# A four-layer decoder trunk: the convolution's diagonal taps issued in halves around the next projection, summed in accumulator banks, and the output weights split after the first statistics

## The chip, the cores and the metric

One core of one Trainium2 chip runs the whole program. The time is the device time of one execution in microseconds (us), as the median of several executions. TensorE is called PE, VectorE DVE, ScalarE ACT, GpSimd POOL and the engine that issues the transfers SP, as in the profile. Each engine takes its own instructions in the order in which they were compiled; between engines there are only semaphores.

## The reference

Four layers, each a token mixer and a feed-forward block, in float32, for 256 positions and 1024 channels. The mixer of layers 0 and 3 is the causal convolution, the only code that the change touches:

```python
def conformer_conv(x, w_in, b_in, w_dw, b_dw, ln_g, ln_b, w_out, b_out):
    h = x @ w_in + b_in
    a, g = jnp.split(h, 2, axis=-1)
    h = a * jax.nn.sigmoid(g)
    h = causal_dwconv(h, w_dw, b_dw)          # 31 taps for each channel
    h = jax.nn.silu(layer_norm(h, ln_g, ln_b))
    return h @ w_out + b_out
```

## The kernel before

Weights come from memory as `raw` tiles of 1 MB (pool of 4) and are split into a high half `whi` (ACT, L87) and a low half `wlo` (DVE, L88), so that PE can make a float32 product out of three faster ones (L105 to L107). PE's order is the order of the source. DVE's, ACT's and SP's is made by a scheduler when the program is built; `tc.issue_after` tells it only that an instruction has to stand behind another.

In `conv` (layer 0 with `j` = 0, layer 3 with `j` = 1) the channels are in four pairs of 128-channel blocks, numbered `pr` = 0 to 3; `n` = 0, 1 is the block inside a pair. For a pair:

- `project(pr)`: 96 products into two PSUM banks, for n = 0 first (gate, then value), then n = 1.
- `glu(pr)`: for each n a sigmoid on ACT (`sg`, L429) and a product on DVE (`chp`, L430), then 16 shifted copies into the tile `h4` (shown as `h`), some on ACT (L422) and some on DVE (L424). `h4` and the diagonal weights `dg` (`diagonals`, DVE, L404) have two buffers each: those of pair 2 are those of pair 0, and those of pair 3 those of pair 1. POOL clears the left border of each `h4` (L413).
- `rest(pr)`: the last 3 to 7 of the 31 taps by plain multiply-add, the first of them on ACT (L446), the others on DVE (L448), into `cv`.
- `taps(pr)`: the other taps as products with diagonal matrices on PE (L461), 24 or 28 for each n (two records each in the trace), and one addition on DVE that puts their sum onto `cv` (L464).
- `to_tokens(pr, t)`: transposes of `cv` on PE (L469) into the accumulator banks `tm`, for token tiles t = 0, 1.

After all four pairs DVE takes the layer norm's statistics (`stats`, L475), and `normalise` (L478), `turn_z` (PE, L483), `activate` and the output product follow for token tile 0 and then 1. Pairs 2 and 3 go through `taps` by token tile. The matrix of the output product is four units `ws`; the first two are loaded and split just before `glu(3)`, the last two after the second statistics. The dictionary `order` holds the last copies of `glu(3)`, behind which later splits stand.

PSUM has eight banks here: four in the rotating pool `mm` (`bank()`), four named accumulators (`acc_bank(t, h)`).

Of the kernel before, what the change touches and what calls it, by code (L numbers as in the profile page):

```python
# [12 lines left out]
AF = mybir.ActivationFunctionType  # L13
# [14 lines left out]
ALPHA = (2 * DEPTH) ** 0.25  # L28
EPS = 1e-5


GROUPS = ((6, 6, 7, 7), (6, 6, 6, 7))
ACT_COPIES = ((11, 16, 12, 9), (7, 15, 13, 8))
GMIN, GMAX = min(map(min, GROUPS)), max(map(max, GROUPS))


@with_exitstack
def trunk(ctx: ExitStack, tc: tile.TileContext, ins, out):
# [18 lines left out]
    def bank():  # L57
        return mmp.tile([P, 512], F32, name="mm", tag="mm")
# [4 lines left out]
    def accs():  # L63
        return [[acc_bank(t, h) for h in range(2)] for t in range(2)]
# [32 lines left out]
    def unit_rows(w, k0, parts=1):  # L97
        return halves(load(w[k0 * P:(k0 + 2) * P, :].rearrange("(k p) n -> p k n", p=P), 2, D), 2, D, parts)
# [264 lines left out]
    def conv(j, prm, lv, turn, nxt, w_first):  # L363


        with tc.tile_pool(name=f"conv{j}", bufs=2) as p:
# [4 lines left out]
            def project(pr, ws=None):  # L371

                parts = 4 if pr == 1 and j == 0 else 1
                ws = ws or conv_weights(j, pr, parts)
                bks = [bank() for n in range(2)]
                if pr:
                    ws = [halves(w, KT, 256, parts) for w in ws]
                    for n in range(2):
                        for s in range(2):
                            proj_cols(bks[n][:, s * T:(s + 1) * T], ws[s], n)  # L380
                    return bks
                for t in range(2):
                    for n, s in ((0, 0), (1, 0), (0, 1)) if t == 0 else ((0, 0), (0, 1), (1, 0)):
                        if (t, n, s) == (1, 1, 0) and j == 0:
                            first["prm"] = prm(acc_bank(1, 1))
                        proj_cols_f32(bks[n][:, s * T:(s + 1) * T], ws[s], n, t, turn if (t, n, s) == (0, 0, 1) else None)
                    if j == 0:
                        proj_cols_f32(bks[1][:, T:], ws[1], 1, t)
                if j:
                    proj_cols(bks[1][:, T:], halves(ws[1][:, :, P:], KT, P), 0)  # L390
                return bks
# [16 lines left out]
            def glu(pr, bks):  # L408

                hp = p.tile([P, 2, PAD + T], F32, name="chp", tag="chp", bufs=3)  # L410
                pool.memset(hp[:, :, 0:PAD], 0.0)
                h4 = p.tile([P, 2, 4, PAD + T], F32, name="h4", tag="h4")
                pool.memset(h4[:, :, :, 0:PAD], 0.0)  # L413
                last = {}

                def copies(a, b):
                    for r in range(4):
                        for s in range(4):
                            src, dst = hp[32 * r:32 * r + 32, a:b, PAD:], h4[32 * s:32 * s + 32, a:b, r, PAD - s:PAD - s + T]
                            i = 4 * r + s  # L420
                            if i * ACT_COPIES[j][pr] // 16 != (i + 1) * ACT_COPIES[j][pr] // 16:
                                last["act"] = act.activation(out=dst, in_=src, func=AF.Identity).ins  # L422
                            else:
                                last["dve"] = dve.tensor_copy(dst, src).ins  # L424

                for n in range(2):
                    c = 2 * pr + n
                    sg = p.tile([P, T], F32, name="sg", tag="sg")
                    act.activation(out=sg, in_=bks[n][:, :T], func=AF.Sigmoid, bias=b_in[:, 8 + c:9 + c])  # L429
                    dve.scalar_tensor_tensor(out=hp[:, n, PAD:], in0=bks[n][:, T:], scalar=b_in[:, c:c + 1], in1=sg, op0=ALU.add, op1=ALU.mult)  # L430
                    if pr == 3:
                        copies(n, n + 1)
                if pr < 3:
                    copies(0, 2)
                return hp, h4, last

            def rest(pr, hp):

                cv = p.tile([P, 2, T], F32, name="cv", tag="cv", bufs=3)
                k0 = 4 * GROUPS[j][pr]  # L440
                for k in range(k0, KW):
                    for n in range(2):
                        c = 2 * pr + n
                        x, w, y = hp[:, n, k:k + T], w_rest[:, (k - 4 * GMIN) * 8 + c:(k - 4 * GMIN) * 8 + c + 1], cv[:, n, :]
                        if k == k0:
                            act.activation(out=y, in_=x, func=AF.Identity, scale=w, bias=b_dw[:, c:c + 1])  # L446
                        else:
                            dve.scalar_tensor_tensor(out=y, in0=x, scalar=w, in1=y, op0=ALU.mult, op1=ALU.add)  # L448
                return cv

            def taps(pr, t0=0, t1=T, ns=(0, 1)):
                if (pr, t0) not in sums:
                    sums[pr, t0] = bank().rearrange("p (n t) -> p n t", n=2)
                ps = sums[pr, t0][:, :, 0:t1 - t0]
                for n in ns:
                    for g in reversed(range(GROUPS[j][pr])):

                        first_g = g == GROUPS[j][pr] - 1
                        a = t0 if first_g else max(t0, PAD - 4 * g - 3)
                        for r in range(4):  # L460
                            pe.matmul(out=ps[32 * r:32 * r + 32, n, a - t0:], lhsT=dg[pr][:, 4 * n + r, g, :], rhs=h4[pr][:, n, r, 4 * g + a:4 * g + t1],  # L461
                                      start=first_g, stop=g == 0)
                y = cv[pr][:, ns[0]:ns[-1] + 1, t0:t1]
                dve.tensor_tensor(out=y, in0=ps[:, ns[0]:ns[-1] + 1, :], in1=y, op=ALU.add)  # L464
# [7 lines left out]

            def stats(t, h):
                with tc.issue_after(order["dve"]):
                    dve.bn_stats(out=st[t][:, h, :], in_=tm[t][h])  # L475

            def normalise(t, h, mv, rs):
                dve.tensor_scalar(out=z[t][:, h * 512:(h + 1) * 512], in0=tm[t][h], scalar1=mv[:, 0:1], scalar2=rs, op0=ALU.subtract, op1=ALU.mult)  # L478
# [19 lines left out]
            hp[0], h4[0], _ = glu(0, b0)  # L498
            cv[0] = rest(0, hp[0])
            b = project(1)  # L500
            tm = accs()
            dg[1] = diagonals(1)
            hp[1], h4[1], _ = glu(1, b)
            cv[1] = rest(1, hp[1])
            taps(0)
            b = project(2)
            for t in range(2):
                to_tokens(0, t)
            lv = lv()
            nxt = nxt()  # L510
            dg[2] = diagonals(2)
            hp[2], h4[2], _ = glu(2, b)
            taps(1)
            b = project(3)
            for t in range(2):
                to_tokens(1, t)
            dg[3] = diagonals(3)
            ws = [unit_rows(wout, 2 * q) for q in range(2)]
            hp[3], h4[3], last = glu(3, b)
            order.update(last)  # L520
            cv[2] = rest(2, hp[2])
            cv[3] = rest(3, hp[3])
            taps(2, 0, P)
            taps(2, P, T, (0,))
            for t in range(2):
                stats(t, 0)
            nxt = nxt()
            to_tokens(2, 0)
            taps(3, 0, P)
# [388 lines left out]
```

## Time and profile before

| | |
|---|---|
| median of 3 executions (1331.25 to 1336.53) | 1332.46 us |
| the profiled execution | 1332.35 us, of which span 1330.4 us |
| PE busy | 1297.1 us, 97% of the span |
| DVE busy | 1038.2 us, 78% |
| ACT busy | 782.2 us, 59% |
| chain that ended last, share of PE | 90% |
| granted clock of PE, mean | 0.993 |

A clock of 1.00 is 2.4 GHz and 0.50 is 1.2 GHz. All times inside the span count from its start: layer 0's convolution is at about 5 to 120 us, layer 3's at about 1027 to 1134 us. A bracket at the end of a timeline row is the idle time of the engine just before it, and what ended it.

### The profile page before, as it was taken

How to read it: one execution, taken by the hardware profiler on the slowest of the kernel's cores; microseconds unless marked ns; L12 is line 12 of the kernel's file. 1: busy time of each engine (PE TensorE's matmuls, PEld its weight loads, DVE VectorE, ACT ScalarE, POOL GpSimd, SP SyncE). 2: the span in 40 equal slices, each digit the busy share in tenths (PEclk: the TensorE clock that was granted, in tenths of full speed). 3: DMA queues.
4: the chain of work that ended last, by engine and by line, in shares of the span. 5: the costliest groups of instructions: out<-in, count | busy, mean ns of one | idle time of the engine just before them, and what ended most of it. 6: DMA issues, size and time to landing. Idle time of an engine off the chain costs nothing.

```text
span 1330.4 us, 21217 instructions
## 1 busy us (share of the span) xinstructions
PE 1297.1 (97%) x8338; PEld 1111.3 (84%) x8338; DVE 1038.2 (78%) x1539; ACT 782.2 (59%) x1138; POOL 56.0 (4%) x251
## 2 busy tenths in 40 slices
PE   8979999999999999999999999999999989999997
PEld 8768888886997988886788888988888977988886
DVE  4968987776686987776779665997777986987776
ACT  4973766653674766662555443676662873666661
POOL 0000000001011000100000000000000000000000
PEclk9989999999999999999999999999999999999999
DMA  7713955553732765553867553665553732665530
GB/s 255 258 48 113 296 193 187 186 182 108 245 121 79 256 205 189 192 190 119 314 221 260 166 191 127 220 216 187 187 190 95 238 128 65 220 216 192 189 134 32
DMA packets 167937, 239.79 MB, mean 180 GB/s; under 512 B 7253, under 2 KB 135838, under 8 KB 167838
## 3 DMA queue, kind: packets, MB, share of 16 engines
q1 hardware_dynamic: 167838, 238.44, 54.2%
q8 instruction: 65, 1.06, 0.3%
q14 instruction: 34, 0.28, 0.1%
HBM read 237.38 MB, written 1.05 MB: 179 GB/s over the span
## 4 chain that ended last, share of the span: by engine, by line
PE 90%; ACT 3%; DVE 3%; DMA 1%; issue 1%; SPq 1%; POOL 0%; DVEq 0%; ACTq 0%; POOLq 0%
PE mm L224 26%; PE mm L225 13%; PE acc L107 9%; PE acc L105 9%; PE acc L106 9%; PE mm L107 5%; PE mm L105 4%; PE mm L106 4%; PE mm L232 4%; ACT h L422 2%; PE mm L461 2%; PE mm L242 2%; PE mm L823 1%; DVE cv L448 1%; PE acc L642 1%
## 5 line engine op out<-in xcount | busy, mean ns | idle before, releaser
L88 DVE TENSOR_TENSOR wlo<-raw,whi 128x2048 fp32r<-128x2048 f32 (+2 forms) x239 | 450.0, 1891 | 128.6 <-ACT whi L87 128.1
L224 PE MATMUL mm<-xT_s,whi 128*128 128x512 f32 x1472 | 516.6, 395 | 0.0
L87 ACT ACTIVATE whi<-raw 128x2048 fp32r<-128x2048 f32 (+2 forms) x239 | 377.3, 1593 | 138.2 <-PE mm L224 77.7
L225 PE MATMUL mm<-xT_s,wlo 128*128 128x256 f32 x1472 | 412.3, 280 | 0.0
L224 PEld LDWEIGHTS mm<-xT_s,whi 128*128 128x128 f32 x1472 | 275.9, 187 | 64.1
L225 PEld LDWEIGHTS mm<-xT_s,wlo 128*128 128x128 f32 x1472 | 277.9, 189 | 1.6
L286 DVE SCALAR_TENSOR_TENSOR y<-hp,prm,y 128x256 f32<-128x256 f32 x352 | 164.6, 479 | 32.2 <-ACT y L281 26.1
L281 ACT ACTIVATE y<-hp,prm 128x256 f32<-128x256 f32 x160 | 94.3, 593 | 109.8 <-DVE hp L280 109.3
L105 PE MATMUL acc<-whi,hh 128*128 128x512 f32 x352 | 139.6, 397 | 0.0
L107 PE MATMUL acc<-whi,hl 128*128 128x512 f32 x352 | 139.5, 396 | 0.0
L106 PE MATMUL acc<-wlo,hh 128*128 128x512 f32 x352 | 139.1, 395 | 0.0
L105 PE MATMUL mm<-xT_s,whi 128*128 128x256 f32 x360 | 103.9, 289 | 0.0
L107 PE MATMUL mm<-xT_s,wlo 128*128 128x256 f32 x360 | 101.9, 283 | 0.0
L106 PE MATMUL mm<-xT_s,whi 128*128 128x256 f32 x360 | 101.8, 283 | 0.0
L279 ACT ACTIVATE hp<-mm,prm 128x256 f32<-128x256 f32 x160 | 74.1, 464 | 13.4 <-PE mm L225 13.4
L107 PEld LDWEIGHTS acc<-whi,hl 128*128 128x128 f32 x352 | 66.1, 188 | 17.3 <-DVE hl L102 1.5
L105 PEld LDWEIGHTS acc<-whi,hh 128*128 128x128 f32 x352 | 66.1, 188 | 15.8
L106 PEld LDWEIGHTS acc<-wlo,hh 128*128 128x128 f32 x352 | 66.1, 188 | 14.2
L232 PE MATMUL mm<-xT,raw 128*128 128x128 f32 x608 | 71.1, 277 | 0.4 <-DMA raw<-in_a_w_in_dram 0.4
L232 PEld LDWEIGHTS mm<-xT,raw 128*128 128x128 f32 x608 | 70.3, 194 | 1.2 <-issue 0.8
L105 PEld LDWEIGHTS mm<-xT_s,whi 128*128 128x128 f32 x360 | 69.0, 192 | 1.6 <-issue 1.5
L107 PEld LDWEIGHTS mm<-xT_s,wlo 128*128 128x128 f32 x360 | 69.0, 192 | 0.2 <-DVE wlo L88 0.2
(162 smaller groups left out, 1665.4 us busy)
## 6 DMA issues: line engine op xcount, KB each, us to landing
raw<-in_f_w_up_dram SPq DMA_DIRECT2D x88, 1024.0 KB
raw<-in_f_w_down_dram SPq DMA_DIRECT2D x44, 1024.0 KB
raw<-in_c_w_in_dram SPq DMA_DIRECT2D x24, 1024.0 KB
raw<-in_a_w_in_dram SPq DMA_DIRECT2D x12, 1024.0 KB
raw<-in_b_w_qkv_dram SPq DMA_DIRECT2D x12, 1024.0 KB
raw<-in_c_w_out_dram SPq DMA_DIRECT2D x12, 1024.0 KB
raw<-in_a_w_out_dram SPq DMA_DIRECT2D x8, 1024.0 KB
raw<-in_b_w_o_dram SPq DMA_DIRECT2D x4, 1024.0 KB
```

Of the source, the lines that this page charges most:

```text
L87: act.activation(out=h, in_=r, func=AF.Identity)
L88: dve.tensor_tensor(out=l, in0=r, in1=h.bitcast(F32), op=ALU.subtract)
L105: pe.matmul(out=ps, lhsT=lh, rhs=rh, start=start, stop=False)
L106: pe.matmul(out=ps, lhsT=lh, rhs=rl, start=False, stop=False)
L107: pe.matmul(out=ps, lhsT=ll, rhs=rh, start=False, stop=stop)
L224: pe.matmul(out=ps, lhsT=wh[:, k, n * P:(n + 1) * P], rhs=xT_hl[:, :, k, :], start=k == 0, stop=False)
L225: pe.matmul(out=ps[:, :T], lhsT=wl[:, k, n * P:(n + 1) * P], rhs=xT_h[:, :, k, :], start=False, stop=k == KT - 1)
L232: pe.matmul(out=ps[:, t * P:(t + 1) * P], lhsT=w[:, k, n * P:(n + 1) * P], rhs=xT[:, t, k, :], start=k == 0, stop=k == KT - 1)
L242: pe.matmul(out=ps, lhsT=xT[:, t, k, :], rhs=ws[k // 4][:, k % 4, :], start=k == 0, stop=k == KT - 1)
L279: act.activation(out=hp[:, 2:], in_=ps[:, T:], func=AF.Identity, bias=b_up[:, c:c + 1])
L281: act.activation(out=yy, in_=hp[:, 2:].rearrange("p (t n) -> p t n", t=2), func=AF.Identity, scale=w2[:, c:c + 1], bias=b_dw[:, c:c + 1])
L286: dve.scalar_tensor_tensor(out=yy, in0=hp[:, d:d + T].rearrange("p (t n) -> p t n", t=2), scalar=w_[:, c:c + 1], in1=yy, op0=ALU.mult, op1 ...
```

## The change

Five things are edited, all in `conv`:

1. `taps(0)` and `taps(1)` are issued in halves: n = 0 before the next projection, n = 1 behind it. Each half has its own addition (L464).
2. The sums of these two pairs stand in accumulator banks (`acc_bank(0, 1)`, `acc_bank(1, 1)`) and not in the pool's; the second halves of `tm` are allocated only when these banks are free again.
3. The first two units of the output matrix are loaded behind `project(3)`, and split only behind the first statistics.
4. `rest(2)` stands ahead of `glu(3)`.
5. Which engine makes which copy is written as a string instead of a formula; letter by letter it is the same choice.

```diff
-                    for r in range(4):
-                        for s in range(4):
...
-                            if i * ACT_COPIES[j][pr] // 16 != (i + 1) * ACT_COPIES[j][pr] // 16:
...
+                    for i, who in enumerate(COPIES[j][pr]):
+                        r, s = i // 4, i % 4
...
+                        if who == "A":
...
                 if (pr, t0) not in sums:
-                    sums[pr, t0] = bank().rearrange("p (n t) -> p n t", n=2)
+                    sums[pr, t0] = (acc_bank(pr, 1) if pr < 2 else bank()).rearrange("p (n t) -> p n t", n=2)
...
             def stats(t, h):
                 with tc.issue_after(order["dve"]):
-                    dve.bn_stats(out=st[t][:, h, :], in_=tm[t][h])
+                    return dve.bn_stats(out=st[t][:, h, :], in_=tm[t][h]).ins
...
             b = project(1)
-            tm = accs()
+            tm = [[acc_bank(t, 0), None] for t in range(2)]
...
-            taps(0)
+            taps(0, ns=(0,))
             b = project(2)
+            taps(0, ns=(1,))
             for t in range(2):
                 to_tokens(0, t)
...
             hp[2], h4[2], _ = glu(2, b)
-            taps(1)
+            taps(1, ns=(0,))
             b = project(3)
+            raws = [load(wout[2 * q * P:(2 * q + 2) * P, :].rearrange("(k p) n -> p k n", p=P), 2, D) for q in range(2)]
+            cv[2] = rest(2, hp[2])
+            taps(1, ns=(1,))
             for t in range(2):
                 to_tokens(1, t)
             dg[3] = diagonals(3)
-            ws = [unit_rows(wout, 2 * q) for q in range(2)]
             hp[3], h4[3], last = glu(3, b)
             order.update(last)
-            cv[2] = rest(2, hp[2])
             cv[3] = rest(3, hp[3])
+            for t in range(2):
+                tm[t][1] = acc_bank(t, 1)
             taps(2, 0, P)
             taps(2, P, T, (0,))
             for t in range(2):
-                stats(t, 0)
+                order["dve"] = stats(t, 0)
+            ws = [halves(raw, 2, D) for raw in raws]
```

What the scheduler made of it shows only in the compiled order. In the changed kernel the lines up to L411 are one higher than before (L88 is L89 there, L404 is L405), while L422 to L490 are the same.

PE, layer 0, from the end of `project(2)` into `taps(1)`. Before:

```order
L105 MATMUL mm<-xT_s,whi 128x256
L106 MATMUL mm<-xT_s,whi 128x256
L107 MATMUL mm<-xT_s,wlo 128x256
L469 MATMUL acc_398<-ident,cv 128x128 x2
L469 MATMUL acc_400<-ident,cv 128x128 x2
L461 MATMUL mm<-h_406,dg 32x256 x4
```

And with the change:

```order
L461 MATMUL acc_443<-h_231,dg 32x237 x4
L461 MATMUL acc_443<-h_231,dg 32x233 x4
L461 MATMUL acc_443<-h_231,dg 32x229 x4
L469 MATMUL acc_398<-ident,cv 128x128 x2
L469 MATMUL acc_399<-ident,cv 128x128 x2
L461 MATMUL acc_656<-h_404,dg 32x256 x4
```

The second half of pair 0's taps has moved in between the projection and the transposes of pair 0, which need its sum; it stands in the accumulator bank `acc_443`.

DVE, layer 0, the same place: the splits of `project(3)`'s weights (`wlo`), the remaining taps of pairs 1 and 2 (`cv<-chp`), the additions (`cv<-mm` or `cv<-acc`). Before:

```order
L88 TENSOR_TENSOR wlo<-raw,whi 128x2048
L448 SCALAR_TENSOR_TENSOR cv<-chp,cprm,cv 128x256
L464 TENSOR_TENSOR cv<-mm,cv 128x512
L448 SCALAR_TENSOR_TENSOR cv<-chp,cprm,cv 128x256
L404 TENSOR_TENSOR dg<-ident_80,cprm 128x1792
L448 SCALAR_TENSOR_TENSOR cv<-chp,cprm,cv 128x256 x3
L430 SCALAR_TENSOR_TENSOR chp<-mm,cprm,sg 128x256
L448 SCALAR_TENSOR_TENSOR cv<-chp,cprm,cv 128x256 x3
L88 TENSOR_TENSOR wlo<-raw,whi 128x2048
L448 SCALAR_TENSOR_TENSOR cv<-chp,cprm,cv 128x256
L88 TENSOR_TENSOR wlo<-raw,whi 128x2048
L448 SCALAR_TENSOR_TENSOR cv<-chp,cprm,cv 128x256
```

And with the change:

```order
L89 TENSOR_TENSOR wlo<-raw,whi 128x2048
L448 SCALAR_TENSOR_TENSOR cv<-chp,cprm,cv 128x256 x4
L430 SCALAR_TENSOR_TENSOR chp<-mm,cprm,sg 128x256
L448 SCALAR_TENSOR_TENSOR cv<-chp,cprm,cv 128x256 x3
L89 TENSOR_TENSOR wlo<-raw,whi 128x2048
L448 SCALAR_TENSOR_TENSOR cv<-chp,cprm,cv 128x256
L464 TENSOR_TENSOR cv<-acc_443,cv 128x256
L448 SCALAR_TENSOR_TENSOR cv<-chp,cprm,cv 128x256
L405 TENSOR_TENSOR dg<-ident_80,cprm 128x1792
L430 SCALAR_TENSOR_TENSOR chp<-mm,cprm,sg 128x256
```

The addition for pair 0's second half and the diagonal weights of pair 2 now stand behind eight remaining taps, the product of `glu(2)` for n = 0 and the second split of `project(3)`; the first split of the output matrix has gone from here.

DVE, layer 0, from the copies of `glu(3)` to the addition of pair 3's first taps (`cv<-mm 128x2x128`, the second such row). Before:

```order
L424 COPY h_837<-chp 32x256 x7
L448 SCALAR_TENSOR_TENSOR cv<-chp,cprm,cv 128x256 x2
L430 SCALAR_TENSOR_TENSOR chp<-mm,cprm,sg 128x256
L424 COPY h_837<-chp 32x256 x7
L475 BN_STATS bnst<-acc_398 128x6
L475 BN_STATS bnst<-acc_400 128x6
L464 TENSOR_TENSOR cv<-mm,cv 128x2x128
L448 SCALAR_TENSOR_TENSOR cv<-chp,cprm,cv 128x256 x2
L464 TENSOR_TENSOR cv<-mm,cv 128x128
```

And with the change:

```order
L424 COPY h_836<-chp 32x256 x14
L464 TENSOR_TENSOR cv<-mm,cv 128x2x128
L475 BN_STATS bnst<-acc_398 128x6
L475 BN_STATS bnst<-acc_399 128x6
L464 TENSOR_TENSOR cv<-mm,cv 128x128
L134 COPY prm<-mm 128x220
L89 TENSOR_TENSOR wlo<-raw,whi 128x2048 x2
L264 TENSOR_TENSOR prm<-prm 128x44
L464 TENSOR_TENSOR cv<-mm,cv 128x2x128
```

The two low halves of the output matrix now stand between the statistics and the addition of pair 3; the copies of `glu(3)` stand in one row for both n. ACT has the same: 18 copies in a row, then four high halves where there were two.

## Rows read from the trace of the kernel before

**Rows 1.** Waits of PE, totals: first convolution (0:127), then the second (1026:1150).
```profile
PE acc L469 <- ACT h L422: 6.0, 1, 6.0
...
PE acc L469 <- DVE cv L464: 5.9, 1, 5.9
```
**Rows 2.** Timeline of PE, layer 0: start us, us, what, xcount.
```profile
38.43 5.05 PE L461 MATMUL mm<-h,dg 128*32 128x256 f32 x90 [1.31 <-ACT h L422]
...
43.41 0.39 PE L105 MATMUL mm<-xT_s,whi 128*128 128x256 f32 x1
...
55.03 0.60 PE L469 MATMUL acc<-ident,cv 128*128 128x128 f32 x4
55.56 5.07 PE L461 MATMUL mm<-h,dg 128*32 128x256 f32 x96
...
77.08 0.50 PE L131 MATMUL mm<-ident,prow 44*128 44x44 f32 x5
83.60 0.69 PE L469 MATMUL acc<-ident,cv 128*128 128x128 f32 x2 [6.01 <-ACT h L422]
```
**Rows 3.** Timeline of ACT, layer 0.
```profile
44.92 10.31 ACT L422 ACTIVATE h<-chp 32x512 f32<-32x512 f32 x16 [0.56 <-DVE chp L430]
...
56.12 3.70 ACT L87 ACTIVATE whi<-raw 128x2048 fp32r<-128x2048 f32 x2
...
63.89 7.74 ACT L422 ACTIVATE h<-chp 32x512 f32<-32x512 f32 x12 [1.42 <-DVE chp L430]
...
79.69 3.86 ACT L422 ACTIVATE h<-chp 32x256 f32<-32x256 f32 x9 [1.10 <-DVE chp L430]
```
**Rows 4.** Timeline of DVE, layer 0.
```profile
55.89 0.49 DVE L448 SCALAR_TENSOR_TENSOR cv<-chp,cprm,cv 128x256 f32<-128x256 f32 x1 [2.23 <-ACT cv L446]
...
60.32 0.48 DVE L448 SCALAR_TENSOR_TENSOR cv<-chp,cprm,cv 128x256 f32<-128x256 f32 x1
...
63.32 0.48 DVE L430 SCALAR_TENSOR_TENSOR chp<-mm,cprm,sg 128x256 f32<-128x256 f32 x1
...
68.25 2.02 DVE L404 TENSOR_TENSOR dg<-ident,cprm 128x1792 f32<-128x1792 f32 x1
...
79.69 2.07 DVE L424 COPY h<-chp 32x256 f32<-32x256 f32 x7
...
88.70 0.42 DVE L464 TENSOR_TENSOR cv<-mm,cv 128x256 f32<-128x256 f32 x1 [2.52 <-PE mm L461]
...
90.56 0.70 DVE L475 BATCH_NORM_STATS2 bnst<-acc 128x6 f32<-128x512 f32 x1
```
**Rows 5.** Stretches, layer 0: busy time of each engine, then PEclk, the granted clock.
```profile
37.00:38.50 1.50, 0.19 (x5) 0.07 (x8) 1.21 (x2) 1.45 (x4) 0.00 (x0) 1.00 1.08 354
...
80.00:82.00 2.00, 0.00 (x0) 0.00 (x0) 1.90 (x7) 1.92 (x6) 0.00 (x0) 0.62 0.02 5
82.00:83.60 1.60, 0.00 (x1) 0.00 (x1) 1.51 (x3) 1.52 (x5) 0.00 (x0) 0.50 0.00 0
...
86.50:87.50 1.00, 1.00 (x32) 0.97 (x28) 0.00 (x0) 1.00 (x1) 0.00 (x0) 0.59 0.00 0
```
**Rows 6.** Timeline of POOL, layer 0.
```profile
60.78 0.30 POOL L413 MEMSET h<- 128x240 f32 x1 [15.01 <-PE mm L461]
```
**Rows 7.** Timelines of PE, ACT and DVE, layer 3.
```profile
1052.94 5.07 PE L461 MATMUL mm<-h,dg 128*32 128x256 f32 x96
...
1086.70 0.60 PE L469 MATMUL acc<-ident,cv 128*128 128x128 f32 x4
...
1093.13 3.44 ACT L422 ACTIVATE h<-chp 32x256 f32<-32x256 f32 x8 [1.10 <-DVE chp L430]
...
1057.41 2.27 DVE L88 TENSOR_TENSOR wlo<-raw,whi 128x2048 fp32r<-128x2048 f32 x1
...
1075.21 0.48 DVE L430 SCALAR_TENSOR_TENSOR chp<-mm,cprm,sg 128x256 f32<-128x256 f32 x1
...
1104.09 0.70 DVE L475 BATCH_NORM_STATS2 bnst<-acc 128x6 f32<-128x512 f32 x1
```

More of the change, by code (lines that the diff above doesn't have):

```diff
@@ L32 @@
 GROUPS = ((6, 6, 7, 7), (6, 6, 6, 7))
-ACT_COPIES = ((11, 16, 12, 9), (7, 15, 13, 8))
+COPIES = (("VAAVAAVAAVAAVAAA", "AAAAAAAAAAAAAAAA", "VAAAVAAAVAAAVAAA", "VAVAVAVAAVAVAVAA"),
+          ("VVAVAVAVVAVAVAVA", "VAAAAAAAAAAAAAAA", "VAAAAVAAAAVAAAAA", "VAVAVAVAVAVAVAVA"))
 GMIN, GMAX = min(map(min, GROUPS)), max(map(max, GROUPS))
@@ L416, in copies @@
                 def copies(a, b):
-                    for r in range(4):
-                        for s in range(4):
-                            src, dst = hp[32 * r:32 * r + 32, a:b, PAD:], h4[32 * s:32 * s + 32, a:b, r, PAD - s:PAD - s + T]
-                            i = 4 * r + s
-                            if i * ACT_COPIES[j][pr] // 16 != (i + 1) * ACT_COPIES[j][pr] // 16:
-                                last["act"] = act.activation(out=dst, in_=src, func=AF.Identity).ins
-                            else:
-                                last["dve"] = dve.tensor_copy(dst, src).ins
+                    for i, who in enumerate(COPIES[j][pr]):
+                        r, s = i // 4, i % 4
+                        src, dst = hp[32 * r:32 * r + 32, a:b, PAD:], h4[32 * s:32 * s + 32, a:b, r, PAD - s:PAD - s + T]
+                        if who == "A":
+                            last["act"] = act.activation(out=dst, in_=src, func=AF.Identity).ins
+                        else:
+                            last["dve"] = dve.tensor_copy(dst, src).ins
                 for n in range(2):
```

## The prediction

> **What bounds the kernel now.** The page first: PE is busy 97% of the span and carries 90% of the chain that ended last, so a change pays only where it removes idle time of PE, and any delay of PE is paid in full. Then PE's waits by stretch: in each convolution one wait stands out, 6.0 us in layer 0 and 5.9 us in layer 3, both at the first transposes of pair 2 [rows 1]. All that the change can remove is there. The timelines of PE, ACT and DVE around them show why PE waits. In layer 0 it has nothing more to do from 77.6 us on [rows 2], while ACT still makes the copies of the last pair, until 83.55 [rows 3]; those copies, not PE, set the end. The stretches show a second price: PE's clock falls to half at 80.5 us, 2.9 us after PE ran dry (the mean of 0.62 between 80 and 82 is a quarter at full speed), and comes back at 87.3, 3.7 us after work began again [rows 5]. Work at half speed for 3.7 us loses 1.85 us.
>
> **What costs nothing.** The string of copies makes the same choice as the formula, letter by letter. PE's products are the same in number and kind. The four banks of the pool are enough before and after, and each accumulator bank that takes a sum is free by then. Two additions of 256 columns instead of one of 512 add some 0.1 us per pair on DVE, which has idle time there (2.2 us before 55.89 [rows 4]). The first two loads of the feed-forward weights wait on SP for buffers that only the late splits free; between these and PE's first use of the weights still lie the statistics and the output product of both token tiles, and SP has only small loads in between. The late splits themselves cost ACT nothing ahead of the copies: they leave a place where ACT then waits for DVE anyway (below).
>
> **Layer 0, step by step.** The first half of `taps(0)` starts at 38.43 as before and is half of 5.07, so `project(2)` starts at 40.9 instead of 43.41; it takes 11.6 us (43.41 to 55.03 [rows 2]) and ends at 52.5, and the second half at 55.0. That is where PE was before, with the same work done. Now come the transposes of pair 0, which before found their sum ready. Now they need the second half's addition, and in the compiled order this stands on DVE behind the tap that waits at 55.89 for ACT's 16 copies and first tap [rows 3, 4], then a product, three taps, a split and one more tap. The same work lay between 55.89 and 60.32 before, and the tap at 60.32 takes 0.4 [rows 4]; the addition takes 0.42 and ends at 61.15. PE idles from 55.2 to 61.2: a new wait of 6.0 us, with everything up to `project(3)` queued behind it. That gap is as long as the old one, so I charge its clock too: 0.5 us of transposes and 2.5 of taps take 1.85 more. `project(3)` starts at 66.05 (before: 60.6) and ends at 77.65, the second half of `taps(1)` at 80.15.
>
> Who waits for that is `glu(3)`. Its copies go into the buffer from which this half of the taps reads, and POOL clears the border first (0.2 us after PE, then 0.3 [rows 2, 6]). So no copy but one starts before 80.65. Before, those of n = 0 were done by then. ACT now makes all 18 from here; at 0.43 us (9 in 3.86) they end at 88.3, not 83.55. The diagonal weights (1.95) and 14 copies of DVE at 0.296 end earlier, at about 87.
>
> Then the moved splits. ACT's first high half ends at 88.3 + 1.85 (two in 3.70 [rows 3]) = 90.15; DVE's two low halves at 2.2 each end at 94.6, a small one 0.2 later, and the addition of pair 3 (0.42) ends at 95.2, where it was at 88.70 to 89.1, without a split ahead of it [rows 4]. Transposes and handover, 0.4: the statistics begin at 95.6, before at 90.56. **Layer 0: +5.0 us.** From there to the layer's end both orders are alike. Without the clock's price the copies end at 86.1 rather than 88.3 (ACT is then ready only a little before PE), which gives +3.1; with low speed over the whole of the 3 us of work, +6.1.
>
> **Layer 3, the same way.** `project(2)` starts at 55.45 (half of 5.07 after 1052.94 [rows 7]; times less 1000 here). Its second unit's low half began at 57.41 and now has an addition and a tap ahead, so it ends at 60.4; PE wants it after a quarter of the projection, at 58.9, and waits 1.5. The projection ends at 60.4 + 8.7 = 69.1, the second half at 71.6. Its addition stands behind the taps of pair 2, which follow the product now at 71.4. Here the moved splits do help: that product was at 75.21 [rows 7] behind two splits, 4.4 us, less some taps that come earlier. After five taps and three more, one waiting for ACT, the addition ends at 74.2. PE idles 2.6 us. Transposes, first half of `taps(1)`: 77.3. `project(3)`: 88.9; before, 86.70. Second half: 91.4, border clear: 91.9. ACT's 16 copies end at 98.8 (before: 1093.13 + 3.44 = 96.57). High half 100.65, statistics done, two low halves 105.1, a copy and the addition 105.9, statistics 106.4 instead of 104.09. **Layer 3: +2.3 us.** If the 2.6 us gap also brings the clock down: +4.2.
>
> **Sum.** 1332.35 + 5.0 + 2.3 = 1339.65, made against the profiled execution (span 1330.4 and 1.95 around it); the median of the runs shown is 0.1 above that. Nothing later absorbs it: after the program's start no transfer appears among PE's waits.
>
> **The rivals.**
>
> *R1, the stalls only move.* If the second half's addition doesn't hold PE in layer 0, `project(3)` ends at 70 and the end is ACT's again. Product at 63.4 (before 63.32 [rows 4], as the diagonals, 1.95 us, now stand where a split of 2.2 stood), 12 copies in 7.74 [rows 3], two sigmoids and three first taps with DVE between them until 76.0, 18 copies to 83.7. The splits then bring the statistics to 91.5: +0.9. With layer 3 as above: 1332.35 + 0.9 + 2.3 = 1335.55. For it: ACT's chain is the same in length. Against it: DVE takes its instructions in order, and the addition's place is compiled.
>
> *R2, faster.* The half behind `project(3)` covers 2.5 of each wait of 6, and what is left is too short for the clock to fall, which gives back 1.85: 2 × 4.35 = 8.7, that is 1323.65. It needs the copies of `glu(3)` to end by 79.2 in layer 0. Against it: 18 copies take 7.7 us, and they may not begin before the very half that is to cover them.
>
> *R3, the clock falls in layer 3 too.* +1.85: 1341.5. For it: the clock fell 2.9 us after PE ran dry, and the new gap is 2.6. Against it: a gap of 1.31 left it at 1.00 [rows 2, 5], and 2.6 is still short of 2.9. The Trainium skill (TensorE: Matmul & The Clock Gate, Part 1) says that the monitor's window runs freely and doesn't start with the work. By that rule the same gap may cost 1.85 in one execution and nothing in another; neither convolution has a gap between 1.4 and 5 us to show it.
>
> **How the numbers follow.** My forecast 0.53, R1 0.25, R3 0.14, R2 0.08. The likeliest gives 1339.65; I say 1339.6. Its own range is 1337.7 (no clock price) to 1341 (low speed over all the work). With R1 below and R3 above, 1335.0 to 1342.0 holds about 0.85. A measurement of this kernel can tell about 0.5%, 6.7 us, from no change: slower begins at 1339.1. The forecast lies 0.5 us above this with some 2 us either way, so about two thirds of its chance and nearly all of R3's count as slower: 0.35 + 0.13 = 0.48. R1 and the rest of the two: 0.44. R2: 0.08.
>
> **What would show it.** Right: in layer 0 a wait of some 6 us at the first transposes (L469) for DVE's addition (L464), near 55 us, and clock 0.5 near 60; no long copies of the last pair before 80; the waits at the transposes of pair 2 down to 1 or 2 us; statistics (third L475) near 95.6, and in layer 3 7.3 us later than before, near 1111.4. Wrong: PE passes from `project(2)` to `project(3)` without a gap, or the copies of `glu(3)` overlap the taps of pair 1, or the addition of pair 3 comes less than 6 us after the last copy.

## The result, and the profile after

The changed kernel takes 1342.03 us (median of 6, 1341.25 to 1343.08); the kernel before, in the same series, 1333.06 (1331.25 to 1336.53). The ratio is 1.0064, interval 1.005 to 1.0077: 0.64% slower, clear of the noise, and 0.03 us beyond the upper end of the forecast's range (1342.0). The profiled execution took 1342.65 us, span 1340.8, which is 10.4 more than before; the forecast had 7.3 more. PE's share of the chain that ended last fell from 90% to 86%.

Where the 10.4 us arise is seen from the starts of DVE's statistics rows (one BATCH_NORM_AGGREGATE for each layer norm and token tile) against the same rows before. They are 5.95 later at the end of layer 0 (312.15 before), 1.74 more are added in layer 1, nothing in layer 2, and 2.72 in layer 3.

Layer 0, timeline of PE after, against [rows 2]; in brackets the idle time before a row and what ended it:
```profile
52.49 2.64 PE L461 MATMUL acc<-h,dg 128*32 128x256 f32 x48
...
60.95 0.90 PE L469 MATMUL acc<-ident,cv 128*128 128x128 f32 x3 [5.56 <-DVE cv L464]
61.78 5.03 PE L461 MATMUL acc<-h,dg 128*32 128x256 f32 x48
...
78.59 2.64 PE L461 MATMUL acc<-h,dg 128*32 128x256 f32 x48
...
96.03 0.66 PE L469 MATMUL acc<-ident,cv 128*128 128x128 f32 x4 [2.94 <-DVE cv L464]
```
At 55.06 PE has done the same work as before at 55.03, and it then idles 5.56 us for an addition (L464). The half of the taps behind it takes 5.03 instead of 2.64: half speed. The stretches show for how long (the number behind the five busy times is the granted clock):
```profile
58.00:60.00 2.00, 0.00 (x0) 0.00 (x0) 2.00 (x1) 0.62 (x2) 0.00 (x0) 1.00 0.00 0
60.00:61.00 1.00, 0.05 (x1) 0.05 (x1) 1.00 (x4) 0.00 (x0) 0.00 (x0) 0.63 0.00 0
61.00:66.00 5.00, 5.00 (x47) 2.60 (x51) 4.58 (x8) 2.24 (x4) 0.00 (x0) 0.50 0.67 213
66.00:67.00 1.00, 1.00 (x13) 0.28 (x6) 0.12 (x1) 0.98 (x3) 0.00 (x0) 0.50 0.00 0
67.00:69.00 2.00, 2.00 (x17) 2.00 (x18) 0.70 (x2) 1.95 (x4) 0.00 (x0) 0.98 0.00 0
```
The clock was still at 1.00 when the gap was nearly 5 us old, at half (1.2 GHz) from about 60.3, and back at 2.4 GHz only at 67, some 6 us after work began again, not after 3.7 as in [rows 5]. Now DVE and ACT, against [rows 3, 4]:
```profile
55.65 0.48 DVE L448 SCALAR_TENSOR_TENSOR cv<-chp,cprm,cv 128x256 f32<-128x256 f32 x1 [4.32 <-ACT cv L446]
...
60.48 0.42 DVE L464 TENSOR_TENSOR cv<-acc,cv 128x256 f32<-128x256 f32 x1
...
91.03 4.49 DVE L89 TENSOR_TENSOR wlo<-raw,whi 128x2048 fp32r<-128x2048 f32 x2 [1.13 <-ACT whi L88]
95.56 0.42 DVE L464 TENSOR_TENSOR cv<-mm,cv 128x256 f32<-128x256 f32 x1
...
96.51 0.70 DVE L475 BATCH_NORM_STATS2 bnst<-acc 128x6 f32<-128x512 f32 x1 [0.22 <-PE acc L469]
```
```profile
63.71 7.73 ACT L422 ACTIVATE h<-chp 32x512 f32<-32x512 f32 x12 [5.09 <-DVE chp L430]
...
81.29 7.76 ACT L422 ACTIVATE h<-chp 32x256 f32<-32x256 f32 x18 [0.91 <-PE acc L461]
```
The addition stands on DVE behind the tap that waited 4.32 us for ACT, and comes at 60.48. No long copy of the last pair starts before 81.29, when the half of pair 1's taps has been read; ACT then makes all 18 in one piece until 89.05. The two low halves (4.49 us, from 91.03) stand ahead of pair 3's addition at 95.56, for which PE waits 2.94. The statistics begin at 96.51, before at 90.56 [rows 4]. PE's waits in this stretch stood at 6.0 us, once, for a copy [rows 1]; now:
```profile
PE acc L469 <- DVE cv L464: 9.9, 4, 5.6
```
Layer 3 after (it enters 7.69 late), PE and DVE, against [rows 7]:
```profile
1068.15 0.39 PE L108 MATMUL mm<-xT_s,wlo 128*128 128x256 f32 x1 [1.31 <-DVE wlo L89]
...
1081.99 0.55 PE L469 MATMUL acc<-ident,cv 128*128 128x128 f32 x3 [2.36 <-DVE cv L464]
...
1107.03 0.44 PE L469 MATMUL acc<-ident,cv 128*128 128x128 f32 x2 [2.32 <-DVE cv L464]
1107.40 5.90 PE L461 MATMUL mm<-h,dg 128*32 128x128 f32 x160
```
```profile
1108.83 4.50 DVE L89 TENSOR_TENSOR wlo<-raw,whi 128x2048 fp32r<-128x2048 f32 x2 [0.46 <-ACT whi L88]
...
1114.49 0.70 DVE L475 BATCH_NORM_STATS2 bnst<-acc 128x6 f32<-128x512 f32 x1
```

### The profile page after: what moved, and what is told of

Its sections match the earlier page's. It is cut to its first block, busy times and chain, and to the rows that moved or that the text cites. A ratio compares the mean times of both kernels' runs of the same rounds, so it can differ in the third digit from the quotient of the medians.

```text
span 1340.8 us, 21218 instructions
## 1 busy us (share of the span) xinstructions
PE 1303.1 (97%) x8338; PEld 1113.0 (83%) x8338; DVE 1038.0 (77%) x1543; ACT 782.3 (58%) x1138; POOL 56.2 (4%) x251
## 3 DMA queue, kind: packets, MB, share of 16 engines
q8 instruction: 65, 1.06, 0.3%
HBM read 237.38 MB, written 1.05 MB: 178 GB/s over the span
## 4 chain that ended last, share of the span: by engine, by line
PE 86%; DVE 5%; ACT 4%; issue 1%; DMA 1%; SPq 1%; POOL 0%; DVEq 0%; ACTq 0%; POOLq 0%
PE mm L225 25%; PE mm L226 13%; PE acc L108 9%; PE acc L106 9%; PE acc L107 9%; PE mm L108 4%; PE mm L106 4%; PE mm L107 4%; PE mm L233 4%; ACT h L422 3%; PE mm L243 2%; DVE cv L448 1%; DVE wlo L89 1%; PE mm L828 1%; PE acc L461 1%
## 5 line engine op out<-in xcount | busy, mean ns | idle before, releaser
L89 DVE TENSOR_TENSOR wlo<-raw,whi 128x2048 fp32r<-128x2048 f32 (+2 forms) x239 | 450.0, 1892 | 130.0 <-ACT whi L88 129.7
L88 ACT ACTIVATE whi<-raw 128x2048 fp32r<-128x2048 f32 (+2 forms) x239 | 377.1, 1593 | 131.4 <-PE mm L225 72.6
```

The lines of the kernel that those rows point to most:

```text
L88: act.activation(out=h, in_=r, func=AF.Identity)
L89: dve.tensor_tensor(out=l, in0=r, in1=h.bitcast(F32), op=ALU.subtract)
```

## The experiments

The first table collects the runs. "Entry" is how much later than before the run came to the row that stands at 55.89 in [rows 4]; it arises before 9 us, mostly where PE waits for the first loads, and not from the edits, which lie behind that. The next three columns give what each stage adds to the shift of the statistics rows (at 312.15, 1028.53 and 1324.46 before). Ratios are against the kernel before in the same series. The column of layer 0 holds the entry too. Less the entry it is +6.19 for the changed kernel, +2.11 for the halves alone, -0.69 for the late splits alone and for the late transposes, and +3.74 for the gap filled. Edits 2 and 4 were not tried by themselves; apart from the program's start, PE's waits of more than 1 us in the changed convolutions are for L464 and once for a low half, none for a bank.

| kernel | median us | ratio, interval | entry | layer 0 | layers 1, 2 | layer 3 |
|---|---|---|---|---|---|---|
| changed | 1342.03 | 1.0064, 1.005 to 1.0077 | -0.24 | +5.95 | +1.74 | +2.72 |
| halves alone | 1336.73 | 1.0028, 1.0015 to 1.004 | +0.82 | +2.93 | +0.02 | -0.08 |
| late splits alone | 1332.67 | 0.9994, 0.9985 to 1.0003 | +0.56 | -0.13 | +0.09 | -0.23 |
| late transposes | 1331.87 | 0.9993, 0.9983 to 1.0002 | +1.50 | +0.81 | +0.02 | -0.14 |
| pair 1 whole | 1338.47 | 1.0042, 1.0027 to 1.0057 | -0.28 | +3.75 | +1.72 | +1.42 |
| gap filled | 1341.16 | 1.0061, 1.0047 to 1.0075 | +0.61 | +4.35 | -0.11 | +4.26 |
| low halves last | 1344.03 | 1.0086, 1.0073 to 1.01 | -0.42 | +5.64 | +1.68 | +5.91 |
| late transposes, low halves last | 1336.72 | 1.0036, 1.0023 to 1.0048 | +1.14 | +3.12 | +1.72 | +1.49 |
| late splits alone, low halves last | 1338.99 | 1.0045, 1.0032 to 1.0059 | +0.67 | +3.32 | +1.70 | +2.77 |
| splits in idle time | 1337.25 | 1.0031, 1.002 to 1.0043 | -0.21 | +1.54 | -0.15 | +1.96 |
| late transposes, splits in idle time | 1329.38 | 0.9969, 0.9958 to 0.998 | +0.47 | -1.60 | +1.73 | -1.06 |
| the same, lambda late | 1326.90 | 0.9956, 0.9944 to 0.9969 | 0.00 | -2.54 | -1.52 | -2.68 |
| turn filled | 1343.28 | 1.0074, 1.0062 to 1.0087 | +0.35 | +5.79 | +0.93 | +4.38 |

**Halves alone** (edits 1 and 2 on the kernel before; splits and `rest(2)` where they were).
```diff
-            taps(0)
+            taps(0, ns=(0,))
             b = project(2)
+            taps(0, ns=(1,))
...
             ws = [unit_rows(wout, 2 * q) for q in range(2)]
```


> The kernel before with the halves of the taps in accumulator banks alone; the feed-forward weights are split where they were, ahead of pair 3. My reading: the halves carry the loss. In layer 0 the first transposes of pair 0 wait 5 to 6 us for the second half's addition, the clock goes to half behind it, and no long copy of the last pair starts before 80; statistics (the fifth aggregate of the trace, at 103.72 before and 109.66 after) 5 to 6 us later than before, layer 3 another 2 to 3, in all 1339 to 1342. Rival: the two low halves ahead of pair 3's addition carry it (the transposes of pair 3 waited 2.94 us for that addition); without them layer 0 loses 3 us or less and the time is 1336 or less.


1336.73: between my reading and the rival. The mechanism is there in full, PE and then DVE:
```profile
62.01 0.90 PE L469 MATMUL acc<-ident,cv 128*128 128x128 f32 x3 [5.56 <-DVE cv L464]
62.84 4.10 PE L461 MATMUL acc<-h,dg 128*32 128x256 f32 x48
```
```profile
91.62 0.43 DVE L464 TENSOR_TENSOR cv<-mm,cv 128x256 f32<-128x256 f32 x1 [1.25 <-PE mm L461]
93.49 0.70 DVE L475 BATCH_NORM_STATS2 bnst<-acc 128x6 f32<-128x512 f32 x1
```
The third projection ends at 78.58, within 0.01 us of the changed kernel (1.06 later entry, 1.06 less for the clock; that these two cancel is luck). But pair 3's addition now waits for PE, not behind splits, and the statistics come 3.02 earlier than after. So the loss in layer 0 is about half the halves, half the splits; my reading that the halves carry it and the rival that the splits do were each half right. Layer 3, for which I expected another 2 to 3, came out level (-0.08): the waits of 2.07 and 2.31 us are there, but behind the second the clock stayed up, and the 160 products took 4.24 us where before, at low clock, they had taken 5.72.

**Late splits alone** (edits 3 and 4 and the new place of the splits; taps undivided).
```diff
-            ws = [unit_rows(wout, 2 * q) for q in range(2)]
...
-                stats(t, 0)
+                order["dve"] = stats(t, 0)
+            ws = [halves(raw, 2, D) for raw in raws]
```


> The kernel before with the late splits alone (and the tap of pair 2 issued ahead); taps undivided. My reading: the splits do no harm where the copies are not held, since DVE is rid of 4.4 us ahead of the copies; layer 0 between -2 and 0 us, layer 3 between -4 and -2 (its last product stood behind both splits), in all 1326 to 1331, with no gap of PE near 55. Rival: the two low halves that stand ahead of pair 3's addition cost as much here as they seem to after (some 3 us per convolution): 1336 or more.


No change, and 1332.67 lies above the expected range. The last copies end at 82.31 (83.55 before), but PE's clock is low there, so the last taps end late anyway (89.33) and the low halves ahead of pair 3's addition cost only the 0.61 us in this row:
```profile
89.95 0.88 PE L469 MATMUL acc<-ident,cv 128*128 128x128 f32 x4 [0.61 <-DVE cv L464]
```
The splits' 3 us exist only together with the halves, where PE reaches the last taps at full speed. The gain that I expected in layer 3 (2 to 4 us) went into the same place: pair 3's addition came at 1102.87, where it stood at 1102.45 before.

**Late transposes** (the changed kernel, one loop moved).
```diff
             taps(0, ns=(1,))
-            for t in range(2):
-                to_tokens(0, t)
...
             cv[2] = rest(2, hp[2])
+            for t in range(2):
+                to_tokens(0, t)
             taps(1, ns=(1,))
```


> The changed kernel with the transposes of pair 0 moved behind the third projection, so that nothing of PE waits for the second half's addition near 55 us. My reading: that wait and the half clock behind it are gone, the third projection ends near 70 instead of 78.6, the copies of the last pair are then set by ACT again; layer 0 +0.5 to +2 instead of +5.94, layer 3 at most +2.7, in all 1334 to 1338. Rival (the buffer and the splits set the end, whatever the gap): layer 0 stays at +4 or more, in all 1340 or more.


1331.87: below the expected range, level with before. The gap near 55 is gone; smaller ones are left, two in layer 0 and the longest of layer 3:
```profile
77.84 0.55 PE L469 MATMUL acc<-ident,cv 128*128 128x128 f32 x3 [3.46 <-DVE cv L464]
78.31 6.12 PE L461 MATMUL mm<-h,dg 128*32 128x128 f32 x168
...
90.90 0.66 PE L469 MATMUL acc<-ident,cv 128*128 128x128 f32 x4 [1.29 <-DVE cv L464]
...
1104.30 0.66 PE L469 MATMUL acc<-ident,cv 128*128 128x128 f32 x4 [2.43 <-DVE cv L464]
```
Behind the first the clock fell (6.12 us for 168 products that take 4.46 at full speed). Layer 0 stands at +0.81, of which 1.50 is the entry: less that, -0.69, where R1 had put this case at +0.9. Layer 3 loses nothing; the clock, which had fallen there before, stayed up in it.

**Pair 1 whole** (the changed kernel with `taps(1)` undivided ahead of `project(3)`).
```diff
-            taps(1, ns=(0,))
+            taps(1)
             b = project(3)
...
-            taps(1, ns=(1,))
```


> The changed kernel with the taps of pair 1 undivided ahead of the third projection; only pair 0 is in halves. The gap near 55 and its clock stay, but the copies of the last pair no longer stand behind a half of taps. My reading: the gap moves all of PE by 5 to 8 us and ACT is late by less, so this gives back 1 to 4 us in layer 0 and 1 to 3 in layer 3: 1335 to 1340. Rival (the held copies cost nothing, the gap alone sets the end): within 1 us of the changed kernel, 1341 to 1343.


As expected: gap and low clock stay (5.55 us; taps 7.03 instead of 5.07), layer 0 gives back 2.20 and layer 3 1.30. Of the 2.20 about 0.9 is a cheaper clock: the same work, third projection and all of pair 1's taps, ended at 80.3 instead of 81.2. The remaining 1.3 is what the held copies cost, at least: in this run the clock fell once more, near 93, in a wait of 2.77 us that it survived in the changed kernel (2.94), and of the 2.46 us gained at layer 0's first aggregate 2.20 are left at its end. In layer 3 the clock fell at the first gap (2.37 us) and not at a later one, the other way round than in the changed kernel, so its 1.30 is not the edit's alone.

**Gap filled** (46 dead products ahead of the first transposes, layer 0 only).
```diff
             taps(0, ns=(1,))
+            if j == 0:
+                warm = bank()
+                for q in range(46):
+                    pe.matmul(out=warm[:, :T], lhsT=xT_h[:, 0, q % KT, :], rhs=xT_h[:, :, q % KT, :], start=True, stop=True)
```


> The changed kernel with 46 added products into a bank that nobody reads, ahead of the first transposes of pair 0 in layer 0 alone: TensorE works through the wait of 5.6 us there. The wait for the second half's addition stays as long; only the clock changes. My reading: no half clock between 60 and 67, the transposes and the half of the taps take 3 us less (0.5 and 2.6 instead of 0.9 and 5.0), and the statistics of layer 0 come about 3 us earlier than in the changed kernel (+3 against before instead of +5.94). If the clock had no part in the loss (rival), they stay at +5.94.


```profile
55.92 5.77 PE L511 MATMUL mm<-xT_s 128*128 128x256 f32 x46
...
62.28 2.64 PE L461 MATMUL acc<-h,dg 128*32 128x256 f32 x48
...
1078.53 0.90 PE L469 MATMUL acc<-ident,cv 128*128 128x128 f32 x3 [2.35 <-DVE cv L464]
1079.36 3.88 PE L461 MATMUL acc<-h,dg 128*32 128x256 f32 x48
```
Layer 0 ends at +4.35 where +3 was expected: 0.85 of it is the later entry, 0.4 another fall of the clock near 96. At the gap itself the reading holds. The half of the taps takes 2.64. The second half of pair 1 starts at 76.54, 2.05 earlier than after, although the run entered 0.86 later: the clock's price at this gap is 2.9 us. In layer 3, where nothing was added, the clock fell behind the gap of 2.35 us (the last row, 3.88 instead of 2.64), which it had not done behind the same gap after. In the profiled execution that ate the gain: the two convolutions together lose 8.61 us, in the changed kernel 8.67. The median, 1341.16, is level with the changed kernel's.

**Low halves last**, in three kernels: the high halves as they are, the first low half behind `normalise(0)`, the second behind token tile 0's activations.
```diff
-            ws = [halves(raw, 2, D) for raw in raws]
...
+            def low(q, ins_):
+                with tc.issue_after(ins_):
+                    dve.tensor_tensor(out=ws[q][1], in0=raws[q], in1=ws[q][0].bitcast(F32), op=ALU.subtract)
...
-                normalise(0, h, mv, rs)
+                done = normalise(0, h, mv, rs)
+            low(0, done)
...
+            low(1, order["dve"])
```


> The kernel with the transposes of pair 0 behind the third projection, and the two low halves of the output weights moved further back: the first behind the normalisation of the first token tile, the second behind its activations. Pair 3's addition then has no split ahead of it. My reading: its wait goes (1.3 us in layer 0, 2.4 in layer 3), the low halves fit into DVE's idle time behind the normalisation (2.3 us) and the activations: layer 0 at -0.5 against before, layer 3 another -2 to -2.5, in all 1328 to 1330.5, faster than both kernels. Rival: the first product of the output waits for its low half instead, and the end stays within 1 us of the kernel without this move, 1331 to 1333.

> The kernel before with the late splits alone, and the two low halves moved further back in the same way. My reading: the late splits gained 1.2 us in layer 0 and about 4 in layer 3 on the copies of the last pair, and lost as much in front of pair 3's addition; with that cost gone the gain shows: layer 0 -1 to -1.5 against before, layer 3 another -1 to -2.5, in all 1328.5 to 1331. Rival: pair 3's addition was not held by the low halves (PE's half clock set it), and the time stays at 1332 to 1333.

> The changed kernel with the two low halves moved further back in the same way and nothing else. My reading: the 2.94 us for which the transposes of pair 3 wait in layer 0 and 0.7 in layer 3 go: layer 0 at +3 against before, as with the halves alone, layer 3 at most +2.7, in all 1337 to 1339. Rival (the late splits are not behind the wait): +5 or more in layer 0, 1341 or more.


All three readings failed on the total: each became slower than the kernel it was made from, by 4.9, 6.3 and 2.0 us of the medians (in the first one's span 2.3 in layer 0, 1.6 in layer 3, and 1.7 of clock in layer 1, below). The gain came where expected: the first aggregate, at 91.29 before and 97.24 after, stood at 92.89 in the third kernel. By the end of layer 0 it was gone. DVE, then PE, in the first of the three:
```profile
92.90 2.28 DVE L538 TENSOR_TENSOR wlo<-raw,whi 128x2048 fp32r<-128x2048 f32 x1
95.09 0.28 DVE L464 TENSOR_TENSOR cv<-mm,cv 128x128 f32<-128x128 f32 x1
...
98.71 0.29 DVE L464 TENSOR_TENSOR cv<-mm,cv 128x128 f32<-128x128 f32 x1 [2.55 <-PE mm L461]
...
99.52 2.28 DVE L538 TENSOR_TENSOR wlo<-raw,whi 128x2048 fp32r<-128x2048 f32 x1
...
104.73 0.20 DVE L146 BATCH_NORM_AGGREGATE mv<-bnst 128x2 f32<-128x12 f32 x1
104.85 2.24 DVE L89 TENSOR_TENSOR wlo<-raw,whi 128x2048 fp32r<-128x2048 f32 x1
107.00 0.15 DVE L138 TENSOR_SCALAR ve<-mv 128x1 f32<-128x1 f32 x1
```
```profile
95.43 3.21 PE L461 MATMUL mm<-h,dg 128*32 128x128 f32 x56 [1.68 <-DVE cv L464]
```
The first low half holds up the addition at 95.09, for which PE waits 1.68, and at that wait the clock falls (the 56 products take 3.21 us, at full speed 1.74). The second (99.52) pushes the two splits of the next units back, and the last of these falls between the second tile's aggregate and its follow-up at 107.00, 2.2 us. The idle time that I had counted on is there (2.31 us before, 2.55 here), but behind that addition, in front of the row at 98.71; in the compiled order the low half stands ahead of the addition.

**Splits in idle time** (first on the changed kernel, then on the one with late transposes): the split issued right behind the loads, its low halves behind DVE's last copy of pair 2.
```diff
-            hp[2], h4[2], _ = glu(2, b)
+            hp[2], h4[2], last = glu(2, b)
...
+            for raw, (hi, lo) in zip(raws, ws):
+                act.activation(out=hi, in_=raw, func=AF.Identity)
+                with tc.issue_after(last["dve"]):
+                    dve.tensor_tensor(out=lo, in0=raw, in1=hi.bitcast(F32), op=ALU.subtract)
...
-            ws = [halves(raw, 2, D) for raw in raws]
```
(The expectations call these the feed-forward output weights; they are the convolution's `wout`.)


> The changed kernel with the feed-forward output weights split in the same early place, and nothing else; the transposes of pair 0 stay where the change has them. My reading: the wait of 5.6 us near 55 and its clock stay, the 2.94 us in front of pair 3's addition go: layer 0 at +2 to +3.5 against before, layer 3 at 0 to +2, in all 1335 to 1339. Rival (the splits' place is not what the second half of the loss hangs on): +5 or more in layer 0, 1340 or more.

> The kernel with the transposes of pair 0 behind the third projection, and the feed-forward output weights split early: the high halves where ACT waits for pair 2's second product (some 5 us), the low halves behind DVE's copies of pair 2, where DVE waits 5.5 us for ACT. My reading: neither pair 3's addition nor the second tile's statistics has a split ahead of it now, so the gain of 0.9 us at layer 0's first statistics that the last version showed is kept, and layer 3 gains the 2.4 us of its wait: 1329 to 1331.5, faster than both kernels. Rival: in layer 3 DVE's idle time is cut in two (1.6 and 4.6 us), so the low halves delay pair 3's first product and its copies, and layer 3 gives back as much: 1332 to 1334.


On the changed kernel the statistics come at 92.12 in place of 96.51: 3.0 us for the splits (as with the halves alone) and 1.4, not expected, because the clock fell and came back sooner (last section). With the transposes late as well, 1329.38 is faster than both kernels, as expected, and the rival's delay of pair 3's copies doesn't show. ACT, then DVE:
```profile
58.74 3.71 ACT L517 ACTIVATE whi<-raw 128x2048 fp32r<-128x2048 f32 x2
...
64.42 7.74 ACT L422 ACTIVATE h<-chp 32x512 f32<-32x512 f32 x12 [1.48 <-DVE chp L430]
```
```profile
66.30 4.49 DVE L519 TENSOR_TENSOR wlo<-raw,whi 128x2048 fp32r<-128x2048 f32 x2
...
87.13 0.42 DVE L464 TENSOR_TENSOR cv<-mm,cv 128x256 f32<-128x256 f32 x1 [1.75 <-PE mm L461]
```
The high halves shorten ACT's wait for the product from 5.09 to 1.48 and the low halves fill DVE's wait for ACT (5.51 with the transposes late and the splits still behind the statistics). The addition waits for PE alone. One loss is left, in layer 1 (+1.73).

**The turn of layer 1.** At the head of layer 1 PE turns the activations by transposes and then waits for DVE's copy of the result. The rows of the first product behind it, before and after, and the clock after:
```profile
320.31 7.13 PE L242 MATMUL mm<-raw,xT 128*128 128x512 f32 x16 [1.91 <-DVE xT L166]
```
```profile
326.27 8.83 PE L243 MATMUL mm<-raw,xT 128*128 128x512 f32 x16 [1.92 <-DVE xT L167]
```
```profile
326.00:328.00 2.00, 1.73 (x3) 0.70 (x4) 1.90 (x4) 1.96 (x4) 0.00 (x0) 0.62 0.01 4
```
The gap is the same, 1.91 and 1.92 us; before, the stretch from 320 to 330 is at 1.00. Two kernels: 14 dead products in the gap of the changed kernel, and, on the fastest version, the gap made short, by putting the lambda chain (the few small steps on DVE and ACT for the layer's scalar lambda) on DVE behind the copy that PE waits for.
```diff
                 if t == 0:
                     turn()
+                    if j == 0:
+                        warm = bank()
+                        for _ in range(14):
+                            pe.matmul(out=warm[:, :P], lhsT=ident, rhs=ident, start=True, stop=True)
```
```diff
-                dve.tensor_tensor(out=lq, in0=lq, in1=lk, op=ALU.mult)
+                with tc.issue_after(order["dve"]):
+                    dve.tensor_tensor(out=lq, in0=lq, in1=lk, op=ALU.mult)
```


> The changed kernel with 14 added products into a bank that nobody reads, in layer 1's turn, where TensorE waits 1.9 us for the transposed activations: the gap is worked through, its length stays. My reading: the 1.74 us that the changed kernel lost there (clock 0.62 and 0.52 in the 4 us behind the gap, where the kernel before kept 1.00) is the clock's alone; with the products the clock stays at 1.00, and layer 1 adds nothing to the +5.9 of layer 0: 1340 to 1341.5, and no time above 1342. Rival: the loss comes from the later order of layer 1's work: +7.7 at the sixth layer norm as before, 1342 to 1343.

> The fastest version so far (transposes of pair 0 behind the third projection, splits in the idle stretches) with layer 1's small lambda chain put behind the copy of the transposed activations on DVE, in front of which it now waits 1.6 us for an exponential of ACT. My reading: TensorE's gap at layer 1's turn falls from 1.9 to some 0.8 us, which gives 1.1, and a gap that short leaves the clock alone, which gives up to 1.7 more where it had fallen: 1326.5 to 1328.5. Rival: the gap is set by the transposes and ACT's own copy, and nothing changes: 1328.5 to 1330.


```profile
324.02 3.29 PE L595 MATMUL mm<-ident 128*128 128x128 f32 x28
327.15 7.03 PE L243 MATMUL mm<-raw,xT 128*128 128x512 f32 x16
...
1081.51 4.32 PE L461 MATMUL acc<-h,dg 128*32 128x256 f32 x48
```
```profile
316.21 7.13 PE L243 MATMUL mm<-raw,xT 128*128 128x512 f32 x16 [0.35 <-DVE xT L167]
```
With the dead products the clock stayed at 1.00 (in six kernels it did so without them, last section, so this one trace doesn't show that they held it), but they took 3.29 us where the gap had 1.9, and 0.93 of the 1.74 remained; and in layer 3 the clock fell behind the gap of 2.38 us (4.32 for 2.64). In the profiled execution these two miss the expected total. The short gap (0.35 us) gained 1.52 against before, in place of the 1.1 expected, with the clock at 1.00; with it the kernel takes 1326.90, the fastest here. In this execution the clock fell in neither convolution, where before it fell in both, so layer 0's -2.54 and layer 3's -2.68 are not all the edits'.

## Why the forecast came out as it did

- **The new wait** was right in place, cause and size: L464 behind the waiting tap, addition done at 60.9 (forecast 61.15), PE idle 5.56 us (6.0).
- **The clock behind it** was right in kind and mis-sized: charged at 1.85, it cost 2.9 (gap filled). The step that failed is the one that carried over the 3.7 us of low speed from [rows 5]; here it was 6. The low clock lasted as long in both, 6.8 us (80.5 to 87.3 before, 60.3 to 67.1 here); but before it fell 2.9 us after PE ran dry, so that PE idled through its first 3.1 us, and here 4.9 us after, so that only 0.7 us of it fell into the wait. Bounding it by "low speed over all the work" (+6.1) had been the better end.
- **The held copies** were right: first copy 81.29 (80.65), the last of ACT 89.05 (88.3). Undoing them returned 1.3 us or more.
- **The moved splits** were right in the sum: 4.4 us forecast, 4.49 measured, addition done at 95.98 (95.2). Their price in this kernel, 3.0 us, is shown by two kernels without them in that place (halves alone, splits in idle time). That alone they cost nothing had not been said.
- **Layer 0** thus came to +5.95 instead of +5.0, and nearly all of the difference is the clock's (less the entry +6.19: 1.2 more than forecast, of which the clock is 1.05).
- **Layer 3**: the wait for the low half 1.31 (1.5), the gap 2.36 (2.6), statistics at 1106.8 less entry (1106.4): +2.7 for +2.3. Here the clock stayed up behind the first gap and fell behind the second (1107.40, 5.90 in place of 4.24), where the splits covered it.
- **Layer 1's 1.74** were in no step. No work of the change lies there and the gap is as before; that the moment of arrival decides is argued, not shown (last section). Of the 3.1 us by which the profiled execution lies beyond the forecast's 7.3, they are more than half; the forecast's range had no term for them.
- **Rivals.** R1's price for layer 0 was met only by luck in the kernel in which its condition holds (late transposes: +0.81 for +0.9), since 1.50 of the 0.81 is the late entry; less that, the copies of the last pair started at 74.7, not at 76.0, and the layer gained 0.69. R1's layer 3, taken over from my forecast, was 2.4 too high there, of which some 1.5 is that the clock stayed up. R2 failed as argued: PE had the cover, the copies could not start. Nor were the 3.5 us that R2 leaves of each wait too short for the clock to fall, by the 2.9 us of the same prediction. R3's mechanism is real. The clock did fall at the first gap of 2.3 to 2.4 us in layer 3 in four kernels (pair 1 whole, gap filled, low halves last, turn filled), and not in the changed one (2.36 us) nor with the splits in idle time (2.43 us). The Trainium skill (TensorE: Matmul & The Clock Gate, Part 1) says that the monitor's window runs freely; these rows agree with it, and do not prove it.
- **Slips in the working:** without the clock's price the copies end at 86.4, not 86.1 (88.3 less 1.85; the +3.1 goes with 86.4); R1's copies, done at 83.7, give statistics at 91.0 and +0.4 by the steps of the forecast, not 91.5 and +0.9; in layer 3 a quarter of the projection ends at 58.35, not 58.9, but the sum goes on from the low half's 60.4 either way.

## What to carry to other kernels

Work put behind a wait as cover is only cover if its result is not wanted next: here the second half's addition stood on DVE behind another wait, and PE ran into it. When work is moved out of one place, look for an engine's idle stretch in the trace (two waits for each other, here 5 us each on ACT and DVE) rather than for "later"; the same splits cost 3 us behind the copies, lost 2 to 6 further back (a part of that to the clock) and were free in the idle stretch. Two edits that seem independent can share one slack: the late splits alone cost nothing, the halves alone 2.9 in layer 0, both 5.95 (less the entry: -0.7, 2.1 and 6.2).

## What was not expected of the hardware

- **The same gap, with and without the clock's price.** At layer 1's turn PE idles 1.8 to 1.9 us in twelve of the profiled kernels. In six of them (before, halves alone, late splits alone, late transposes, gap filled, splits in idle time) the granted clock stays at 1.00; in the other six it falls to half, and the 16 products behind it take 8.83 us instead of 7.13 where a trace shows them in one row. The changed kernel's six times lie in two groups, 1341.3 and 1342.9, some 1.5 apart; that this is the same coin thrown in each execution is argued, not shown: each kernel has one profile, the mean granted clocks on record don't tell the two groups apart (0.992 to 0.995 in the slower, 0.993 to 0.995 in the faster), and the entry alone differs by 1.9 us among the profiles. The plainest pair is the wait of 3.46 us in front of pair 1's transposes in layer 0: behind it the 168 products took 6.12 us with late transposes (row at 78.31 there), and 4.46 in the fastest kernel:
```profile
76.34 0.55 PE L469 MATMUL acc<-ident,cv 128*128 128x128 f32 x3 [3.46 <-DVE cv L464]
76.82 4.46 PE L461 MATMUL mm<-h,dg 128*32 128x128 f32 x168
```
  In all fourteen traces together, after the first 20 us, PE waited 1.6 to 3.5 us 45 times; the clock fell during 25 of these waits or just behind them, and at all twelve waits of more than 4 us.
- **The low clock lasted as long, but fell sooner or later.** Behind the gap of 5.5 to 5.6 us at 55 the half of the taps (2.64 at full speed) took 5.03, 4.10, 4.00, 3.75 and 3.78 us in five kernels with the same work there (changed, halves alone, low halves last, splits in idle time, turn filled). In each of them the clock was at half for 6.8 us. What differs is when it fell: 4.9 us after PE ran dry in the changed kernel, 2.6, 2.4, 1.9 and 1.9 us in the others, so that less of the low stretch was left for the work behind the wait. With the splits in idle time, where PE waits from 55.40 to 60.98, it fell at 57.3 and was back at 64.1; the clock is 0.50 between these two rows:
```profile
57.00:58.00 1.00, 0.00 (x0) 0.00 (x0) 0.96 (x3) 1.00 (x2) 0.00 (x0) 0.64 0.03 10
...
64.00:65.00 1.00, 1.00 (x26) 0.56 (x21) 0.97 (x4) 0.99 (x2) 0.00 (x0) 0.94 0.54 209
```
  A forecast can carry such a price only as a range.
